# Stick-breaking attention: log(1+e^z) taken from e^z directly, with a cap, and the casts of two weight pieces moved from DVE to ACT

## The chip, the cores and the metric

The kernel runs on one core of a Trainium2 chip, in one launch. The metric is the device time of one execution in microseconds (us). Five engines matter: PE multiplies matrices and writes PSUM banks, ACT evaluates functions and copies, DVE and POOL do elementwise arithmetic (POOL on SBUF alone), and SP issues the DMA transfers. Each engine works through its own instructions in order.

## The reference, cut to what matters

One inference step of a two-layer trunk over 512 prompt frames and 64 sample frames, with a model width of 1024: first a convolution layer with its feed-forward part, then a layer of stick-breaking attention (16 query heads, 4 key/value heads) with its feed-forward part. The change lies in the attention:

```python
z = jnp.einsum('bgrqd,bgsd->bgrqs', q, k) * (HEAD_DIM ** -0.5)
mask = k_pos[None, :] < q_pos[:, None]
log_beta = jax.nn.log_sigmoid(z)
log_keep = jnp.where(mask, log_beta - z, 0.0)
after = lax.cumsum(log_keep, axis=4, reverse=True) - log_keep
att = jnp.where(mask, jnp.exp(log_beta + after), 0.0)
out = jnp.einsum('bgrqs,bgsd->bgrqd', att, v)
```

Here log_keep is -log(1+e^z), so every score needs s = log(1+e^z), then a sum of s over the later keys, then an exponential.

## The kernel before

Everything is float32. Matrices are multiplied as sums of two rounded parts: an operand x becomes hi (x rounded to the matrix engine's own 32-bit format, a copy or cast) and lo (x minus hi), and PE multiplies both. So each tensor that PE reads costs one cast and one subtraction.

The attention stage is cut into 10 pairs of heads (8 of prompt queries, 2 of sample queries), each pair into 2 units, each unit into 3 pieces of keys. That is 20 units and 60 pieces. In a prompt unit (16 of them) the pieces are 384 columns (in a 512-wide tile), 384 and 512 columns wide; in a sample unit (4 of them) they are 512, 512 and 256. A piece goes through these stages:

- `stage_z`: PE writes the scores z and the mask (-1e30) into one of five PSUM banks (L2105, L2110; tile `b`).
- `stage_s`: ACT and DVE make s in a buffer `t` (`zt` for the first prompt piece), L2130 to L2139; then `parts` makes hi and lo of it (tiles `s`, `zs`): the cast at L2070 on ACT, the subtraction at L2076 on DVE. For piece 0, POOL also adds two key blocks (`as`, L2154), which are split in turn (`a`).
- `stage_t`: PE adds the sums of s over later keys onto z in the same bank (L2177).
- `stage_e`: ACT takes the exponential (L2190) and the bank is free; then hi by a cast on DVE (L2072; tiles `e`, `ze`) and lo (L2076) on DVE for pieces 0 and 1 and on POOL for piece 2.
- `stage_v`: PE multiplies with the values (L2205); ACT and DVE collect the output `oc` (L2218, L2221).

Between these, PE has projections to do (L587): queries for later pairs (`pq`) and, late in the stage, the first half of the output projection (`pw`). Their weights arrive by SP (L309, buffers `wr`), and are split by ACT (L505) and DVE (L515). The split queries of a pair (`qd`, L1988 on ACT, L1992 on POOL) are spread over the partitions by SP: two transfers for the second unit (L2005) into a buffer whose last reader on PE has to be done, then one for the first unit (L2009).

The order on every engine is set by a planner (`Plan`). Each operation is entered with an engine, a cost and the keys that it reads and writes; a list scheduler places all of the section's operations and writes the instructions out in that order. So an operation that changes engine or goes away moves others on all engines of the section.

Of the kernel before, what the change touches and what calls it, by code (L numbers as in the profile page):

```python
# [6 lines left out]
AF = mybir.ActivationFunctionType  # L7
ALU = mybir.AluOpType
E = mybir.EngineType

P = 128
D = 1024
NC = D // P
SEQ = 512
# [59 lines left out]
LT, LV = 1, 2  # L74
W_LO = "DVE"
Q_LO = "Pool"
S_HI, E_HI = "ACT", "DVE"
E_LO = ("DVE", "DVE", "Pool")
A_LO = "Pool"

# [25 lines left out]
class Plan:  # L106
# [19 lines left out]
    def op(self, eng, cost, fn, reads=(), writes=(), lat=0.0, group=None, bias=0.0, urgent=False, port=False):  # L126
        i, deps = len(self.ops), set()
        for k in reads:
            if k in self.w:
                deps.add(self.w[k])  # L130
            self.r.setdefault(k, []).append(i)
        for k in writes:
            deps.update(self.r.pop(k, ()))
            if k in self.w:
                deps.add(self.w[k])
            self.w[k] = i
        deps.discard(i)
        self.ops.append((eng, cost, fn, deps, lat, group, bias, urgent, port or eng == "Pool"))
        self.end.append(0.0)
# [75 lines left out]
def build(tc, xT, vec, st, stp, bdp, wt, ck, cv, w_in, w_out, gu, down, wk, wv, wq, wo, yT, csp, css, kp, ks, vp, vs):  # L215
    nc = tc.nc
# [87 lines left out]
    X = {}  # L304
# [32 lines left out]
    op = plan.op  # L337
# [8 lines left out]
    def tile(key, tag, shape, dt=F32, pool=None):  # L346
        X[key] = (pool or cur[0]).tile(list(shape), dt, name="_".join(map(str, key)), tag=tag)
        return X[key]
# [4 lines left out]
    def act(n, scaled=True):  # L353
        return 0.186 + n * 0.000834 if scaled else 0.16 + n * 0.000715

    def dve(n, ptr=False):
        return n / 960 + (0.13 if ptr else 0.07)

    def pool(n):
        return 0.15 + n * 0.0021  # L360
# [4 lines left out]
    def both(k):  # L365
        return [k, (k, 0), (k, 1)]
# [187 lines left out]
    def eng(e):  # L554
        return nc.vector if e == "DVE" else nc.gpsimd

    def cst(e, n):
        return dve(n) if e == "DVE" else pool(n)
# [1287 lines left out]
    for t in range(2):  # L1846
        ft, ht, lt = (("ob0", "ob1", "ob2"), ("ob3", "ob0", "ob1"))[t]
        wi = take()
        tag = (("b0", "b1"), ("b2", "b3"))[t]
# [197 lines left out]
    def slot(q, first):  # L2047

        if first:

            i, j = turn["z" + q] % N_Z[q], turn["zt"] % N_Z["t"]
            turn["z" + q] += 1
            turn["zt"] += 1
            return ("z", q, i), f"z{q}{i}", ("z", "t", j), f"zt{j}"
        key, tag = (q, turn[q]), f"h{q}{turn[q] % N_HL[q]}"
        tk, tt = ("t", turn["t"]), (("sq1",) + tuple(f"t{i}" for i in range(N_T - 1)))[turn["t"] % N_T]
        turn[q] += 1
        turn["t"] += 1
        return key, tag, tk, tt

    def place(key, tag, shape, dt=F32):
        return X[key] if key[0] == "z" else tile(key, tag, (P, 5 * P) if tag == "sq1" else shape, dt, base if tag == "sq1" else None)

    def parts(key, tag, tk, tt, sl, le, he="DVE"):
        n = sl.stop - sl.start

        def hi():
            o = place(key, tag, (P, 2, 256 if key[0] == "a" else SEQ), F32R)[:, 0, sl]
            if he == "ACT":
                nc.scalar.activation(o, X[tk][:, sl], AF.Copy)  # L2070
            else:
                nc.vector.tensor_copy(o, X[tk][:, sl])  # L2072

        def lo():
            q = X[key]
            eng(le).tensor_tensor(q[:, 1, sl], X[tk][:, sl], q.bitcast(F32)[:, 0, sl], op=ALU.subtract)  # L2076

        if he == "ACT":
            op("ACT", act(n, False), hi, reads=[tt], writes=both(tag))
        else:  # L2080
            op("DVE", 0.08 + n / 1920, hi, reads=[tt], writes=both(tag), port=True)
        op(le, cst(le, n), lo, reads=[tt, (tag, 0)], writes=[(tag, 1)], port=True)
# [5 lines left out]
    def stages(un):  # L2088
# [30 lines left out]
        def cols(pi):  # L2119
            first = un.kind == "p" and pi == 0  # L2120
            sl = slice(P if first else 0, piece_cols(un.pieces[pi]))
            return first, sl, sl.stop - sl.start

        def stage_s(pi):
            first, sl, n = cols(pi)
            zz, zk = z[pi]
            key, tag, tk, tt = slot("s", first)

            def f():
                nc.scalar.activation(place(tk, tt, (P, SEQ))[:, sl], zz()[:, sl], AF.Abs)  # L2130

            def g():
                nc.scalar.activation(X[tk][:, sl], X[tk][:, sl], AF.Exp, scale=-1.0)

            def s():
                nc.scalar.activation(X[tk][:, sl], X[tk][:, sl], AF.Ln, bias=1.0)

            def v():
                nc.vector.scalar_tensor_tensor(X[tk][:, sl], zz()[:, sl], 0.0, X[tk][:, sl], op0=ALU.max, op1=ALU.add)  # L2139

            op("ACT", act(n, False), f, reads=[zk], writes=[tt])
            op("ACT", act(n, False), g, reads=["tbl"], writes=[tt])
            op("ACT", act(n, False), s, reads=["tbl"], writes=[tt])
            op("DVE", dve(n, True), v, reads=[zk], writes=[tt])
            parts(key, tag, tk, tt, sl, "DVE", S_HI)
            for (b, o, q0, q1) in un.pieces[pi]:
                sp.append((b, o, q0, q1, key, tag))
            if pi == 0:

                ak, atag, sk = ("a", turn["a"]), f"ha{turn['a'] % N_A}", ("as", turn["a"])  # L2150
                turn["a"] += 1

                def a():
                    nc.gpsimd.tensor_tensor(tile(sk, "as", (P, 256)), X[tk][:, 0:256], X[tk][:, 256:512], op=ALU.add)  # L2154

                op("Pool", pool(256), a, reads=[tt], writes=["as"])
                parts(ak, atag, sk, "as", slice(0, 256), A_LO)
                later.append((ak, atag))
# [25 lines left out]
        def stage_e(pi):  # L2184
            first, sl, n = cols(pi)
            zz, zk = z[pi]
            key, tag, tk, tt = slot("e", first)

            def f():
                nc.scalar.activation(place(tk, tt, (P, SEQ))[:, sl], zz()[:, sl], AF.Exp)  # L2190

            op("ACT", act(n, False), f, reads=[zk, "tbl"], writes=[tt])
            parts(key, tag, tk, tt, sl, E_LO[pi], E_HI)
            for (b, o, q0, q1) in un.pieces[pi]:
                at[pi].append((b, o, q0, q1, key, tag))

        def stage_v(pi):
# [30 lines left out]
            for (j, a, b, o) in jobs:  # L2228
# [24 lines left out]
                op("Pool", pool(b - a), lo, reads=[("oc", 0), ("oc", 1)], writes=[fk + (a,)])  # L2253

        return [stage_z, stage_s, stage_t, stage_e, stage_v]

    def prepare(i):
# [54 lines left out]
    n = len(todo)  # L2312
    fill = iter(range(NC))
    for s in range(n + LV):
        if 0 <= s - LT < n:
            st, pi, _, _ = todo[s - LT]
            st[2](pi)
            st[3](pi)
        if 0 <= s - LV < n:
            st, pi, _, _ = todo[s - LV]  # L2320
            st[4](pi)
        if s < n:
            st, pi, ahead, i = todo[s]
# [114 lines left out]
```

## Time and profile before

| what | value |
|---|---|
| time, median of 3 runs | 1265.24 us (1264.75 to 1266.52) |
| the profiled execution's own time | 1266.71 us |
| its span, first to last instruction | 1265.0 us |
| mean granted PE clock | 0.994 of full |
| busy over the span | PE 97%, DVE 79%, ACT 77%, POOL 60% |
| attention stage, first score matmul to the last values | 661.4 to 842.7 us |

The profile shows one execution. "Busy" counts time in which an engine has an instruction in work; matmuls overlap in PE's pipeline, so that a busy PE can still be short of instructions. A wait of an engine costs time only where that engine, or one behind it, sets the end.

### The profile page before, as it was taken

To read this page: it belongs to the slowest core of one execution; us is meant where nothing else is said; L and a number is where in the kernel's file an instruction comes from. 1 tells how busy PE (TensorE), PEld (TensorE's weight loads), DVE (VectorE), ACT (ScalarE), POOL (GpSimd) and SP (SyncE) were. 2 spreads that over 40 slices of the span, in tenths; PEclk is the share of its full clock that TensorE was granted. 3 is DMA by queue.
4 is the path that set the end of the run, shared out by engine and by line. 5 is a ranking of instruction groups with operands and counts; after the bars stand their busy time and mean duration, and the time that the engine had idled before them with its cause. 6 is when DMAs were issued, how large, how long until landed. Compare 5 with 4: busy or idle time off the path is not lost.

```text
span 1265.0 us, 24386 instructions
## 1 busy us (share of the span) xinstructions
PE 1229.3 (97%) x9018; PEld 1202.7 (95%) x9018; DVE 997.7 (79%) x1619; ACT 975.5 (77%) x1882; POOL 762.0 (60%) x638
## 2 busy tenths in 40 slices
PE   8999899999999999999999999999999999999996
PEld 7998889999999999999999989898999999999996
DVE  6997957977666659987789999999866666689976
ACT  6986236588878889687759999965988788896873
POOL 4988122459877777664304555555686777867633
PEclk9999999999999999999999999999999999999999
DMA  5333222132423323232363222231323233232322
GB/s 189 93 110 105 71 66 84 51 101 68 130 70 102 100 83 100 74 113 85 123 166 98 47 59 63 60 110 50 101 73 127 69 98 103 80 99 79 112 67 76
DMA packets 46455, 115.61 MB, mean 91 GB/s; under 512 B 8832, under 2 KB 18112, under 8 KB 46336
## 3 DMA queue, kind: packets, MB, share of 16 engines
q1 hardware_dynamic: 46336, 114.05, 29.6%
q8 instruction: 71, 1.16, 0.4%
q14 instruction: 48, 0.39, 0.1%
HBM read 99.04 MB, written 6.34 MB: 83 GB/s over the span
## 4 chain that ended last, share of the span: by engine, by line
PE 71%; DVE 8%; ACT 3%; issue 2%; POOL 2%; DMA 1%; DVEq 0%; SPq 0%; POOLq 0%; ACTq 0%
PE j_A L1396 26%; PE j_B L1396 13%; PE pd L587 7%; PE j_C L1396 6%; PE pq L587 4%; PE po L587 4%; PE b L2177 2%; PE pw L587 2%; PE b L2110 1%; PE b L2205 1%; PE pg L587 1%; PE pv L1925 1%; PE pk L587 1%; DVE wl L515 1%; DMA wr<-gu 1%
## 5 line engine op out<-in xcount | busy, mean ns | idle before, releaser
L505 ACT ACTIVATE wh<-wr 128x512 fp32r<-128x512 f32 (+1 forms) x303 | 183.2, 612 | 37.9 <-PE po L587 15.2
L515 DVE TENSOR_TENSOR wl<-wr,hp 128x512 fp32r<-128x512 f32 (+1 forms) x241 | 158.5, 662 | 53.1 <-ACT hp L510 52.5
L515 DVE TENSOR_TENSOR wl<-S,hp 128x512 fp32r<-128x512 f32 x226 | 152.4, 680 | 42.1 <-ACT hp L510 39.5
L505 ACT ACTIVATE wh<-S 128x512 fp32r<-128x512 f32 x228 | 140.8, 626 | 31.8 <-PE pd L587 10.4
L510 ACT ACTIVATE hp<-wr 128x512 fp32r<-128x512 f32 (+1 forms) x241 | 138.9, 578 | 30.6 <-DVE wl L515 30.1
L510 ACT ACTIVATE hp<-S 128x512 fp32r<-128x512 f32 x226 | 133.6, 594 | 13.9 <-POOL S L435 8.9
L435 POOL TENSOR_TENSOR S<-wr,wr 128x512 f32<-128x512 f32 x57 | 76.9, 1350 | 87.5 <-ACT wh L505 39.8
L471 POOL TENSOR_TENSOR S<-wr,S 128x512 f32<-128x512 f32 x57 | 78.4, 1377 | 32.4 <-DVE wl L515 18.0
L435 POOL TENSOR_TENSOR S<-wr 128x512 f32<-128x512 f32 x57 | 78.7, 1381 | 30.7 <-DVE wl L515 13.2
L1059 POOL TENSOR_TENSOR pacc<-pacc,pr 128x608 f32<-128x608 f32 x56 | 83.8, 1503 | 10.5 <-ACT pr L1056 3.9
L435 POOL TENSOR_TENSOR S<-S,wr 128x512 f32<-128x512 f32 x57 | 78.0, 1370 | 15.1 <-DVE wl L515 6.9
L1573 POOL TENSOR_TENSOR a<-a,r 128x576 f32<-128x576 f32 x44 | 66.9, 1522 | 15.6 <-DVE a L1550 15.6
L1573 POOL TENSOR_TENSOR t<-t,r 128x576 f32<-128x576 f32 x44 | 65.6, 1494 | 9.8 <-ACT t L1544 8.5
L587 PE MATMUL pd<-ap,wh 128*128 128x288 f32 x384 | 66.0, 294 | 0.0
L1579 DVE TENSOR_TENSOR a<-a,t 128x576 f32<-128x576 f32 x44 | 51.3, 1166 | 7.5 <-ACT t L1577 6.8
L587 PEld LDWEIGHTS pd<-ap,wh 128*128 128x128 f32 x384 | 56.0, 188 | 0.0
L515 DVE TENSOR_TENSOR wl<-wr,wh 128x512 fp32r<-128x512 f32 x62 | 48.5, 789 | 8.7 <-ACT wh L505 8.5
L1042 DVE SCALAR_TENSOR_TENSOR acc<-u,vecs,acc 128x608 f32<-128x608 f32 x60 | 51.1, 852 | 1.0
L1544 ACT ACTIVATE t<-j_A 128x288 f32<-128x288 f32 x84 | 34.0, 405 | 21.9 <-PE j_A L1396 21.5
L934 PE MATMUL py<-vt,wm 128*128 128x152 f32 x288 | 41.3, 307 | 5.2 <-DVE ye L944 5.2
L934 PEld LDWEIGHTS py<-vt,wm 128*128 128x128 f32 x288 | 40.4, 201 | 6.0 <-DVE ye L944 5.8
L1056 ACT ACTIVATE pr<-u,vecs 128x608 f32<-128x608 f32 x56 | 42.9, 793 | 3.9 <-POOL pacc L1059 3.8
(859 smaller groups left out, 4567.7 us busy)
## 6 DMA issues: line engine op xcount, KB each, us to landing
wr<-gu SPq DMA_DIRECT2D x88, 512.0 KB, 3.4
wr<-down SPq DMA_DIRECT2D x32, 512.0 KB, 3.7
wr<-w_in SPq DMA_DIRECT2D x15, 512.0 KB, 3.9
wr<-down SPq DMA_DIRECT2D x16, 384.0 KB, 3.1
qd<-qd SPq DMA_DIRECT2D x21, 256.0 KB, 3.5
wr<-w_out SPq DMA_DIRECT2D x8, 512.0 KB, 3.5
wr<-wq SPq DMA_DIRECT2D x8, 512.0 KB, 3.7
wr<-wo SPq DMA_DIRECT2D x16, 256.0 KB, 2.6
```

The source lines that it names most:

```text
L435: eng(e).tensor_tensor(t[:, :n], x[1](), y[1](), op=ALU.subtract if sub else ALU.add)
L471: eng(e).tensor_tensor(v[:, :n], X[("raw", i0)][:, n : 2 * n], v[:, :n], op=ALU.subtract)
L505: nc.scalar.activation(X[("w", u)][0][:, :n], get(), AF.Copy)
L510: nc.scalar.activation(t[:, :n], get(), AF.Copy)
L515: eng(le).tensor_tensor(b[:, :n], get(), a.bitcast(F32)[:, :n], op=ALU.subtract)
L587: nc.tensor.matmul(o[hf], (hi, hi, lo)[j][:, s], (xh, xl, xh)[j], start=(start and q == 0 and j == 0), stop=(stop and q == n - 1 and j == 2),)
L934: nc.tensor.matmul(X[("py", c)][:, YO + q * QW : YO + q * QW + QW], X[("wm", c, q)][:, Q * j : Q * j + Q, :].rearrange("p j d -> p (j d)") ...
L1042: nc.vector.scalar_tensor_tensor(dst, src, wt_, dst, op0=ALU.mult, op1=ALU.add)
L1059: nc.gpsimd.tensor_tensor(X[("pacc", c)], X[("pacc", c)], X[("pr", c, i)], op=ALU.add)
L1396: nc.tensor.matmul(out, a[:, s], b, start=(start and q == 0 and i == 0), stop=(q == len(ops_) - 1 and i == 2), skip_group_check=True,)
L1573: nc.gpsimd.tensor_tensor(X[k], X[k], r, op=ALU.mult)
L1579: op("DVE", dve(T), lambda: nc.vector.tensor_tensor(X[ku], X[ku], X[kg], op=ALU.mult), reads=by_part(tg), writes=by_part(tu), port=True)
```

## The change

Before, s was formed as max(z, 0) + log(1 + e^-|z|), with ACT passes for the absolute value, for the exponential and for the logarithm. Now ACT takes e^z straight from the bank, then log(1 + e^z), and DVE forms max(min(that, 15), z). The DVE instruction stays one instruction of the same kind with its inputs exchanged. Second, the casts of the attention weights (hi of `e`) go to ACT for pieces 0 and 1 and stay on DVE for piece 2. The casts of s stay on ACT.

```diff
--- before.py
+++ after.py
@@ -74,7 +74,9 @@
 LT, LV = 1, 2
 W_LO = "DVE"
 Q_LO = "Pool"
-S_HI, E_HI = "ACT", "DVE"
+S_HI = ("ACT", "ACT", "ACT")
+E_HI = ("ACT", "ACT", "DVE")
+SOFT = 15.0
 E_LO = ("DVE", "DVE", "Pool")
 A_LO = "Pool"
 
@@ -2126,23 +2128,20 @@
             zz, zk = z[pi]
             key, tag, tk, tt = slot("s", first)
 
+
             def f():
-                nc.scalar.activation(place(tk, tt, (P, SEQ))[:, sl], zz()[:, sl], AF.Abs)
-
-            def g():
-                nc.scalar.activation(X[tk][:, sl], X[tk][:, sl], AF.Exp, scale=-1.0)
+                nc.scalar.activation(place(tk, tt, (P, SEQ))[:, sl], zz()[:, sl], AF.Exp)
 
             def s():
                 nc.scalar.activation(X[tk][:, sl], X[tk][:, sl], AF.Ln, bias=1.0)
 
             def v():
-                nc.vector.scalar_tensor_tensor(X[tk][:, sl], zz()[:, sl], 0.0, X[tk][:, sl], op0=ALU.max, op1=ALU.add)
-
-            op("ACT", act(n, False), f, reads=[zk], writes=[tt])
-            op("ACT", act(n, False), g, reads=["tbl"], writes=[tt])
+                nc.vector.scalar_tensor_tensor(X[tk][:, sl], X[tk][:, sl], SOFT, zz()[:, sl], op0=ALU.min, op1=ALU.max)
+
+            op("ACT", act(n, False), f, reads=[zk, "tbl"], writes=[tt])
             op("ACT", act(n, False), s, reads=["tbl"], writes=[tt])
             op("DVE", dve(n, True), v, reads=[zk], writes=[tt])
-            parts(key, tag, tk, tt, sl, "DVE", S_HI)
+            parts(key, tag, tk, tt, sl, "DVE", S_HI[pi])
             for (b, o, q0, q1) in un.pieces[pi]:
                 sp.append((b, o, q0, q1, key, tag))
             if pi == 0:
@@ -2190,7 +2189,7 @@
                 nc.scalar.activation(place(tk, tt, (P, SEQ))[:, sl], zz()[:, sl], AF.Exp)
 
             op("ACT", act(n, False), f, reads=[zk, "tbl"], writes=[tt])
-            parts(key, tag, tk, tt, sl, E_LO[pi], E_HI)
+            parts(key, tag, tk, tt, sl, E_LO[pi], E_HI[pi])
             for (b, o, q0, q1) in un.pieces[pi]:
                 at[pi].append((b, o, q0, q1, key, tag))
 
```

The planner then orders the attention stage anew. Ahead of the stage and behind it the instructions stand as before, but for a few casts and projection blocks at its edges (line numbers shift by 2).

On DVE, early in the stage, around the first casts of the weights, before (`zt`, `t` are work buffers, `q` the queries):

```order
L2139 SCALAR_TENSOR_TENSOR zt_7935<-b_8486,zt_7935 128x384
L2072 CAST ze_7934<-zt_7936 128x384
L2076 TENSOR_TENSOR ze_7934<-zt_7936,ze_7934 128x384
L1974 SCALAR_TENSOR_TENSOR q_8625<-pq_0_8510,r 128x288
L1974 SCALAR_TENSOR_TENSOR q_8625<-pq_1_8511,r 128x288
L2076 TENSOR_TENSOR zs_7933<-zt_7935,zs_7933 128x384
L2072 CAST e_8645<-t_8634 128x384
L2072 CAST a_8648<-as_8610 128x256
L2076 TENSOR_TENSOR e_8645<-t_8634,e_8645 128x384
L2139 SCALAR_TENSOR_TENSOR t_8607<-b_8353,t_8607 128x384
```

The same place on DVE after the change:

```order
L517 TENSOR_TENSOR wl_8599<-wr_8397,wh_8598 128x512
L2078 TENSOR_TENSOR zs_7933<-zt_7935,zs_7933 128x384
L2078 TENSOR_TENSOR ze_7934<-zt_7936,ze_7934 128x384
L2139 SCALAR_TENSOR_TENSOR t_8623<-t_8623,b_8567 128x384
L2074 CAST a_8647<-as_8604 128x256
L2078 TENSOR_TENSOR s_8649<-t_8623,s_8649 128x384
L2139 SCALAR_TENSOR_TENSOR t_8645<-t_8645,b_8473 128x512
L2074 CAST e_8676<-t_8666 128x512
L2078 TENSOR_TENSOR e_8669<-t_8634,e_8669 128x384
```

The casts of `ze` and of the 384-column `e` are gone from DVE; the subtraction behind each stays, and now reads what ACT has cast. The cast of the 512-column `e` (piece 2) is still there.

On PE, before the scores of the first prompt pair behind the first sample pair (`qd_9363` are its queries, `kst` the keys, `sums` the triangular matrices), before:

```order
L587 MATMUL pq_0_9451<-xh_80_8214,wh_8948 128x288
L587 MATMUL pq_1_9452<-xh_80_8214,wh_8948 128x288
L587 MATMUL pq_0_9451<-xl_80_8215,wh_8948 128x288
L587 MATMUL pq_1_9452<-xl_80_8215,wh_8948 128x288
L587 MATMUL pq_0_9451<-xh_80_8214,wl_8949 128x288
L587 MATMUL pq_1_9452<-xh_80_8214,wl_8949 128x288
L2177 MATMUL b_8478<-a_9416,sums 128x256 x2
L2177 MATMUL b_8478<-s_9418,sums 128x256 x4
L2177 MATMUL b_8478<-s_9445,sums 128x256 x2
L2105 LDWEIGHTS identb
L2105 MATMUL b_8451<-mask,identb 128x256
L2110 MATMUL b_8451<-qd_9363,kst_7919 128x256 x4
```

The same place on PE after the change (its queries are `qd_9339`):

```order
L589 MATMUL pq_0_9388<-xh_80_8324,wl_9147 128x288
L589 MATMUL pq_1_9389<-xh_80_8324,wl_9147 128x288
L2112 MATMUL b_8567<-qd_9163,kst_7918 128x256 x2
L589 MATMUL pq_0_9388<-xh_80_8334,wh_9146 128x288
L589 MATMUL pq_1_9389<-xh_80_8334,wh_9146 128x288
L589 MATMUL pq_0_9388<-xl_80_8335,wh_9146 128x288
L589 MATMUL pq_1_9389<-xl_80_8335,wh_9146 128x288
L589 MATMUL pq_0_9388<-xh_80_8334,wl_9147 128x288
L589 MATMUL pq_1_9389<-xh_80_8334,wl_9147 128x288
L2107 LDWEIGHTS identb
L2107 MATMUL b_8473<-mask,identb 128x256
L2112 MATMUL b_8473<-qd_9339,kst_7919 128x256 x4
```

Before, one query projection block (6 matmuls `pq`) stands between the last score matmuls of the sample pair's first unit, after which a buffer is refilled for this pair, and these scores; now seven blocks (42) do, of which the rows show the end.

On SP, in the second half of the stage, before (L2005 and L2009 spread queries, L309 loads weights):

```order
L2005 DMA qd_9397<-qd_9363 64x1024 x2
L2009 DMA qd_9363<-qd_9363 64x1024
L309 DMA wr_9510<-wo 128x512
L2005 DMA qd_9606<-qd_9570 64x1024 x2
L2009 DMA qd_9570<-qd_9570 64x1024
L309 DMA wr_9734<-wo 128x512
L2005 DMA qd_9846<-qd_9819 64x1024 x2
L2009 DMA qd_9819<-qd_9819 64x1024
```

The same stretch on SP after the change (L2007 and L2011 spread queries, L311 loads weights):

```order
L311 DMA wr_9494<-wo 128x512
L311 DMA wr_9519<-wo 128x512
L2007 DMA qd_9577<-qd_9531 64x1024 x2
L2011 DMA qd_9531<-qd_9531 64x1024
L311 DMA wr_9633<-wo 128x512
L311 DMA wr_9773<-wo 128x512
L2007 DMA qd_9843<-qd_9733 64x1024 x2
L311 DMA wr_9859<-wo 128x512
L2011 DMA qd_9733<-qd_9733 64x1024
```

Two weight loads now stand ahead of each of these two spreads, and one stands between the two parts of the second (L2007 and L2011). A load between the two parts happens at two spreads of the stage; before, it happened at none.

## Rows read from the trace of the kernel before

**Rows 1.** Busy us of each engine (instructions) before, in and behind the attention stage.

```profile
0.00:661.40 661.40, 646.35 (x4742) 635.96 (x4742) 505.57 (x782) 481.59 (x885) 390.23 (x337) 0.99 0.32 99
661.40:845.00 183.60, 178.07 (x1253) 165.17 (x1252) 176.62 (x333) 166.88 (x354) 99.84 (x94) 1.00 0.26 66
845.00:1265.00 420.00, 404.89 (x3027) 401.53 (x3025) 315.48 (x506) 327.07 (x643) 271.93 (x208) 0.99 0.28 90
```

**Rows 2.** The same by stretches: length, PE, PEld, DVE, ACT, POOL, PE clock, DMA.

```profile
680.00:700.00 20.00, 20.00 (x140) 18.32 (x140) 19.04 (x33) 19.14 (x41) 11.72 (x12) 1.00 0.19 41
700.00:720.00 20.00, 19.97 (x137) 18.44 (x136) 19.10 (x37) 19.26 (x44) 12.02 (x12) 1.00 0.27 61
720.00:740.00 20.00, 17.60 (x119) 15.75 (x118) 19.94 (x37) 19.50 (x43) 10.69 (x11) 1.00 0.23 53
740.00:760.00 20.00, 19.75 (x145) 18.48 (x146) 19.22 (x37) 18.35 (x42) 9.88 (x10) 1.00 0.28 66
800.00:820.00 20.00, 18.28 (x137) 17.18 (x136) 19.80 (x38) 17.84 (x39) 8.70 (x8) 1.00 0.30 71
820.00:845.00 25.00, 24.18 (x174) 23.02 (x173) 24.81 (x52) 17.57 (x35) 15.98 (x15) 1.00 0.23 70
```

**Rows 3.** PE's groups by form, 661 to 845 us: first and last of 19.

```profile
L587 PE MATMUL pw<-ob,wh 128*128 128x288 f32 x141 | 24.6, 296 | 0.0
...
L2105 PE MATMUL b<-mask,identb 128*128 128x256 bf16 x20 | 5.6, 279 | 2.8 <-ACT t L2190 2.7
```

**Rows 4.** The chain that ended last: start us, us, what.

```profile
650.37 11.20 PE pq L587 x84
...
731.16 1.46 POOL qd L1992
732.64 0.48 SPq L2005
733.16 3.67 DMA qd<-qd
736.90 2.88 DMA qd<-qd
739.83 0.73 PE b L2110 x4
```

**Rows 5.** DVE's casts of the weights in the stage: busy us, mean ns.

```profile
L2072 DVE CAST e<-t 128x512 fp32r<-128x512 f32 x24 | 12.6, 533 | 0.2 <-ACT t L2190 0.2
...
L2072 DVE CAST ze<-zt 128x384 fp32r<-128x384 f32 x16 | 8.5, 532 | 1.2 <-ACT zt L2190 0.6 <-PE b L2205 0.6
...
L2072 DVE CAST e<-t 128x384 fp32r<-128x384 f32 x16 | 7.3, 458 | 0.0
```

**Rows 6.** The casts of L2072 on DVE: min/median/max ns.

```profile
L2072 DVE CAST e<-t x44: 286/414/1653, 674.5 to 838.0; 128x512 fp32r<-128x512 f32 x24, 128x384 fp32r<-128x384 f32 x16, 128x256 fp32r<-128x256 f32 x4
```

**Rows 7.** ACT's groups in the stage: busy us, mean ns of one, idle before.

```profile
L2133 ACT ACTIVATE t<-t 128x512 f32<-128x512 f32 (+2 forms) x44 | 24.6, 570 | 0.2
L2130 ACT ACTIVATE t<-b 128x512 f32<-128x512 f32 (+2 forms) x44 | 23.3, 537 | 3.2 <-PE b L2110 2.0 <-DVE s L2076 0.9
L2190 ACT ACTIVATE t<-b 128x512 f32<-128x512 f32 (+2 forms) x44 | 23.0, 535 | 3.0 <-PE b L2177 2.3 <-POOL e L2076 0.6 <-DVE e L2076 0.2
L505 ACT ACTIVATE wh<-wr 128x512 fp32r<-128x512 f32 x23 | 14.2, 628 | 1.3 <-PE pw L587 1.2
...
L2133 ACT ACTIVATE zt<-zt 128x384 f32<-128x384 f32 x16 | 8.4, 524 | 0.1
...
L2070 ACT ACTIVATE zs<-zt 128x384 fp32r<-128x384 f32 x16 | 8.3, 521 | 0.0
```

**Rows 8.** Who waited for whom, 655 to 850 us: total us, times, longest us.

```profile
PE b L2105 <- ACT t L2190: 2.7, 4, 1.7
...
DVE s L2076 <- ACT s L2070: 1.7, 4, 0.5
```

**Rows 9.** What SP's queue waited for, 640 to 850 us: total, times, longest.

```profile
SPq L309 <- DVE wl L515: 73.9, 18, 8.9
```

## The prediction

> **What bounds the kernel now.** I first read the busy time by stage. PE is busy for 178.07 of the 183.60 us of the attention stage, DVE for 176.62 and ACT for 166.88 [rows 1]. So all three are nearly full there, and PE's own work is the least that the stage can take. The change touches no other stage, so the question is how much of the stage PE spends waiting, and for whom.
>
> Two readings bound that. By the busy time PE is idle for 183.60 - 178.07 = 5.5 us. That is too little, since matmuls overlap in the pipeline and a late one hides. The other reading counts the work. The 19 groups of matmuls in the stage, of which the first and the last are shown [rows 3], hold 1256 matmuls with 374,912 columns in all (count times width, added up). Undisturbed, 84 matmuls of 288 columns took 11.20 us [rows 4], that is 133 ns each or 0.463 ns a column. 374,912 x 0.463 = 173.6 us of work, in 184 us: 10.4 us without work. So between 5.5 and 10.4 us can be had here, and no more, as long as PE does the same matmuls.
>
> Then I looked for the place of the waits, by stretches of the stage [rows 2]. Three stretches lose PE time: 720 to 740 us (2.40 of 20), 800 to 820 (1.72 of 20) and 820 to 845 (0.82 of 25). In the same three DVE is full: 19.94, 19.80 and 24.81 us. In the three others shown DVE is at 19.04 to 19.22 of 20, and PE loses 0.00, 0.03 and 0.25 us. The clock is granted in full in all of them. So PE runs dry where DVE has no slack left. The reader should see that 96% of DVE is harmless and 99% is not: pieces pile up in front of it until PE has used up its projections.
>
> **What the change takes away and adds.** There are 60 pieces, 20 each of numbers 0, 1 and 2.
>
> On ACT one pass per piece goes. The remaining exponential reads the PSUM bank, as the absolute value did. From a bank, the absolute value takes 537 ns and the exponential 535 ns in the same mix of sizes [rows 7], so this exchange costs nothing. What goes is the exponential within SBUF, L2133: 24.6 + 8.4 = 33.0 us [rows 7]. What comes is 40 casts: 32 of 384 columns at 521 ns, which is the price of the like cast of s, and 8 of 512 columns at 628 ns, the price of the like cast of weights [rows 7]. That is 16.7 + 5.0 = 21.7 us. ACT falls by 11.3 us, from 166.9 to 155.6.
>
> On DVE 40 casts go: the 16 of `ze` (8.5 us), the 16 of `e` with 384 columns (7.3 us), and 8 of the 24 with 512 columns at 533 ns (4.3 us) [rows 5]. That makes 20.1 us. It is the upper bound, because these durations hold delays: the casts of `e` have a median of 414 ns and a longest of 1653 ns [rows 6]. If the delays only move to other instructions, 40 x 0.414 = 16.6 us go. DVE comes to 156.5 to 160.0 of 183.6 us. I take the first, since a delay goes with the instruction that has it. The instruction that joins s with z stays one pass with its inputs exchanged. No row shows it in this form. The least is no change; as the most I take the excess of mean over median of the cast, 533 - 414 = 119 ns, on all 60: 7.1 us. Even then DVE does 13.0 us less than now. I take nothing for it, since the sizes and the number of inputs are the same.
>
> The subtraction behind each moved cast must now wait for another engine. The nearest row is the same hand-over for s: over 60 of them DVE waited 1.7 us in all, at most 0.5 at once [rows 8]. 40 more give 1.1 us. They cost nothing while DVE has other work in hand; with 20 us less to do it has idle time for them. Queued behind such a subtraction are the joins and subtractions of the next pieces, for which PE's sums wait.
>
> A piece's way through its bank gets shorter by one pass of 570 ns [rows 7], so the bank comes free earlier. PE waited 2.7 us for banks that the second exponential had not freed, in 4 waits [rows 8].
>
> The planner also moves PE's fillers. The loss at 720 to 740 us ends with a chain that no lighter DVE shortens: POOL's part of the queries 1.46 us, SP 0.48, two transfers of 3.67 and 2.88 us in a row, then the scores at 739.83 [rows 4]. Between the release of that buffer and these scores PE had 6 projection matmuls and now has 42. The 36 more are 36 x 133 ns = 4.8 us of cover, against 2.40 us lost. No matmul is added, so this only takes cover from places that did not need it.
>
> The Trainium skill, in its page "ScalarE: Activation LUTs", section "Rules for kernel authors", sends simple elementwise work to VectorE instead of ScalarE. That speaks against moving casts. By that rule alone the casts are dearer than before; this trace agrees on the price of one (521 against 414 ns), and the second rival below says what would come of it.
>
> **The sum.** With DVE at 156.5 of 183.6 us (85%), the stage should look like the three stretches where DVE has slack: 0.28 us of PE lost in 60 us, so 0.9 us in the stage. Of the 5.5 us of visible idle time, 4.6 come back. Of the hidden 10.4 - 5.5 = 4.9 us, I cannot say from a row how much is waiting and how much is the pace of mixed matmuls, so none and all are the bounds, and I take half, 2.4 us. Together 7.0 us. The profiled execution took 1266.71 us, of which 1265.0 are its span and 1.7 lie around it; it would take 1259.7. The median of the runs is 1.5 us lower, and gives 1265.24 - 7.0 = **1258.2 us**. With all the hidden time it is 1254.8, with none 1260.6: this case's own range.
>
> **The rivals.**
>
> PE's waits are not DVE's making. The three losing stretches could lose to the spread of queries and to hand-overs, with DVE full by coincidence. For it speaks the chain at 731 to 740 us, which is POOL, SP and transfers [rows 4]. Against it speaks that the two other losing stretches have DVE at 99% too, and that the spread now has more cover. Then only the loss at the end of the stage, 0.8 us, comes back: 1264.4 us.
>
> ACT's dearer casts land on the way. Each moved cast takes 521 instead of 414 ns and stands in ACT's queue ahead of exponentials that free banks. If all 40 delay PE by the difference, and the hand-overs too, 40 x 0.107 + 1.1 = 5.4 of the 7.0 us are lost: 1263.6 us. Against it: ACT as a whole falls from 91% to 85% of the stage.
>
> SP gets in the way, and the kernel gets slower. At two spreads a weight load now stands between the transfers for the second unit and the one for the first, in the order shown for SP. A load waits until DVE has split the buffer's last content; the longest such wait was 8.9 us [rows 9]. The last transfer would wait for the earlier ones anyway, 3.67 us [rows 4]. That leaves 5.2 us at each place, 10.5 at both: 1258.2 + 10.5 = 1268.7 us. It decides from 3.5 us a place on, that is when the split ends 7.2 us or more after the first transfers start. Against it: most of the 73.9 us in these waits are a queue that is early, not DVE that is late [rows 9], and DVE gets lighter.
>
> **Chances and range.** The forecast 0.72; waits not of DVE's making 0.14; ACT's casts 0.05; SP 0.09. The first holds because three stretches agree on one sign. About 0.2%, or 2.5 us, is what a measurement of this kernel can tell from no change: below 1262.7 is faster, above 1267.8 slower. Faster is the forecast and 0.04 of the second case, where a part of the idle time comes back: 0.76. Same is the rest of it, ACT's case, and 0.01 of SP's where one place is covered: 0.16. Slower 0.08. The range goes from the lower bound of the forecast, 1254.5 with a little for rounding, up past ACT's case to 1264.0; it leaves out SP's case and 0.1 of the second.
>
> **What the profile after would show.** Right: DVE busy in the stage at 156 to 164 us and ACT at about 156; no stretch with DVE at 99%; PE's idle time in the stage near 1 us; the last matmul with the values some 7 us earlier; the stages before and behind as long as now. The step on ACT is wrong if an exponential from a bank is not near 535 ns; the step on DVE if the joining instruction has grown, or the subtractions take up what the casts leave. The prediction fails as a whole if DVE gets its slack and PE still waits, which would show in the same places as waits for transfers or for ACT.

## The result, and the profile after

The changed kernel takes 1257.03 us (median of 5 runs, 1254.52 to 1257.78) against 1265.24 us. The ratio is 0.9924, with a 95% interval of 0.9913 to 0.9936: 8.2 us faster in the medians, 9.6 us (8.1 to 11.0) by the ratio. The profiled execution took 1257.46 us with a span of 1255.7 us, 9.3 us under the span before.

The stages of the profile after, with the columns of [rows 1]; the last matmul with the values now ends at 833.3 instead of 842.7 us, so the stage is cut at 836:

```profile
0.00:661.40 661.40, 648.37 (x4754) 638.75 (x4754) 506.81 (x785) 482.12 (x885) 388.95 (x337) 0.99 0.33 100
661.40:836.00 174.60, 173.15 (x1244) 163.28 (x1243) 161.21 (x290) 157.65 (x335) 94.58 (x94) 1.00 0.27 65
836.00:1255.70 419.70, 404.77 (x3024) 401.23 (x3023) 316.97 (x506) 326.04 (x642) 271.46 (x208) 0.99 0.29 91
```

The gain lies in the attention stage: what stands behind it takes as long as before. PE's idle time in the stage went from 5.5 to 174.60 - 173.15 = 1.45 us. Counted as in the prediction, its 22 groups of matmuls hold 372,320 columns, at 0.463 ns each 172.4 us of work in 175 us: 2.6 us without work, against 10.4.

The stretches of the stage after, with the columns of [rows 2]:

```profile
700.00:720.00 20.00, 18.83 (x131) 17.40 (x130) 17.71 (x31) 17.73 (x40) 10.37 (x10) 1.00 0.29 64
720.00:740.00 20.00, 20.00 (x151) 19.28 (x150) 18.96 (x34) 18.64 (x40) 11.64 (x11) 1.00 0.22 52
740.00:760.00 20.00, 20.00 (x152) 18.88 (x152) 19.94 (x35) 18.84 (x42) 11.46 (x11) 1.00 0.36 92
...
800.00:820.00 20.00, 20.00 (x153) 19.18 (x152) 19.72 (x36) 18.90 (x40) 8.51 (x10) 1.00 0.20 48
```

PE no longer loses anything at 720 to 740 or at 800 to 820 us. But the reader should see the row of 740 to 760 us: DVE is full again, 19.94 of 20 us, and PE loses nothing. A full DVE alone does not make PE wait. The one loss left inside, at 700 to 720 us, is a spread of queries, as the chain of that stretch shows (start us, us, what):

```profile
699.83 5.31 DMA qd<-qd
...
705.20 2.84 DMA qd<-qd
...
708.09 0.74 PE b L2112 x4
```

The groups of the stage after that answer to [rows 5, 7]: of DVE, then of ACT (two fences, since they are two views).

```profile
L2139 DVE SCALAR_TENSOR_TENSOR t<-t,b 128x512 f32<-128x512 f32 x24 | 16.3, 680 | 0.7 <-ACT t L2136 0.6
...
L2078 DVE TENSOR_TENSOR e<-t,e 128x384 fp32r<-128x384 f32 x16 | 12.6, 787 | 0.1
...
L2078 DVE TENSOR_TENSOR ze<-zt,ze 128x384 fp32r<-128x384 f32 x16 | 10.6, 662 | 0.9 <-ACT ze L2072 0.7 <-PE b L2176 0.2
```

```profile
L2133 ACT ACTIVATE t<-b 128x512 f32<-128x512 f32 x24 | 14.3, 594 | 2.9 <-PE b L2112 2.6
...
L2072 ACT ACTIVATE ze<-zt 128x384 fp32r<-128x384 f32 x16 | 8.4, 526 | 0.4 <-PE b L2204 0.3
L2072 ACT ACTIVATE e<-t 128x384 fp32r<-128x384 f32 x16 | 8.4, 522 | 0.1
...
L2072 ACT ACTIVATE e<-t 128x512 fp32r<-128x512 f32 x8 | 4.8, 632 | 0.5 <-PE b L2204 0.5
```

The casts on ACT cost 21.6 us, the joining instruction on DVE is as long as it was (680 ns for 512 columns, before and after), and the subtractions behind the moved casts have grown. So has one that is behind none of them: that of `s` with 384 columns went from 573 to 758 ns in the mean.

### The profile page after: what moved, and what is told of

Its sections match the earlier page's. It is cut to its first block, busy times and chain, and to the rows that moved or that the text cites. A ratio compares the mean times of both kernels' runs of the same rounds, so it can differ in the third digit from the quotient of the medians.

```text
span 1255.7 us, 24378 instructions
## 1 busy us (share of the span) xinstructions
PE 1226.3 (98%) x9018; PEld 1203.3 (96%) x9018; DVE 985.0 (78%) x1579; ACT 965.8 (77%) x1862; POOL 755.0 (60%) x638
## 4 chain that ended last, share of the span: by engine, by line
PE 78%; DVE 6%; issue 1%; ACT 1%; POOL 1%; DMA 1%; DVEq 0%; SPq 0%; POOLq 0%; ACTq 0%
PE j_A L1398 28%; PE j_B L1398 14%; PE j_C L1398 7%; PE pd L589 7%; PE pq L589 4%; PE po L589 4%; PE b L2176 4%; PE pw L589 2%; PE b L2112 2%; PE b L2204 2%; PE pg L589 1%; PE pv L1927 1%; PE pk L589 1%; DVE wl L517 1%; DVE xs L1498 1%
## 5 line engine op out<-in xcount | busy, mean ns | idle before, releaser
L517 DVE TENSOR_TENSOR wl<-wr,wh 128x512 fp32r<-128x512 f32 x62 | 51.3, 836 | 9.1 <-ACT wh L507 8.9
```

What stands on the lines that cost most here:

```text
L517: eng(le).tensor_tensor(b[:, :n], get(), a.bitcast(F32)[:, :n], op=ALU.subtract)
```

## The experiments

The theory of the prediction was that lighter engines, DVE above all, take PE's waits away. The rival that the result left standing was that the planner's new order does it, with its cover for the spread of queries: the two came together in one change. A second question was which of the two edits counts. All kernels were timed in 5 rounds; the kernel before took 1265.7 to 1265.9 us beside them. The table has for each the attention stage from the first mask matmul to the last with the values, in its profile: length, PE's idle time in it, and the busy shares of DVE and ACT (the row of the changed kernel is that of the result).

| kernel | us | ratio to before (95%) | stage us | PE idle us | DVE | ACT |
|---|---|---|---|---|---|---|
| before | 1265.24 | 1 | 181.3 | 5.5 | 96% | 91% |
| changed | 1257.03 | 0.9924 (0.9913 to 0.9936) | 171.9 | 1.5 | 92% | 91% |
| e1 new log alone | 1264.06 | 0.9988 (0.998 to 0.9997) | 174.8 | 2.4 | 96% | 82% |
| e2 casts alone | 1273.13 | 1.0064 (1.005 to 1.0078) | 188.8 | 9.3 | 88% | 96% |
| e3 new work, old order | 1265.74 | 1.0007 (0.9999 to 1.0016) | 180.3 | 5.0 | 89% | 87% |
| e4 old work, new order | 1277.62 | 1.0099 (1.0085 to 1.0113) | 191.0 | 14.1 | 91% | 89% |
| e5 all casts on ACT | 1257.76 | 0.9936 (0.9922 to 0.995) | 174.2 | 1.6 | 90% | 95% |
| e6 new order, casts on DVE | 1269.45 | 1.0032 (1.0019 to 1.0045) | 182.3 | 6.9 | 96% | 78% |
| e7 new order, third pass | 1280.02 | 1.0115 (1.0101 to 1.0129) | 193.4 | 17.4 | 81% | 96% |
| e8 changed, other plan | 1259.26 | 0.9952 (0.9939 to 0.9965) | 173.1 | 1.8 | 95% | 90% |
| e8 before, other plan | 1267.43 | 1.0012 (1.0003 to 1.0021) | 182.3 | 6.6 | 97% | 91% |
| e9 changed, one round | 1262.47 | 0.9967 (0.9955 to 0.998) | 175.7 | 3.0 | 94% | 89% |
| e9 before, one round | 1269.55 | 1.0028 (1.0018 to 1.0038) | 184.1 | 9.5 | 95% | 90% |

The stage lengths are not of quite the same work, since a plan can move query projections over the stage's edge: it holds 1236 matmuls in the kernel before, in e3, in e5 and in e8 before, 1242 in e2, and 1223 or 1224, some 1.6 us less than 1236, in the others.

### e1 and e2: one edit alone, planned anew

e1 is the changed kernel with

```diff
-E_HI = ("ACT", "ACT", "DVE")
+E_HI = ("DVE", "DVE", "DVE")
```

> Only the log(1+e^z) part; all casts of the weights stay on DVE, and the planner orders the stage for that. ACT loses 60 passes (33 us of the stage), DVE keeps its 177 us. If DVE's load made PE wait, this gives little: 1262 to 1265 us, with DVE still at 99% in stretches where PE loses time. If ACT's passes, or the length of a piece's way through its bank, made PE wait, it gives most of the gain: 1257 to 1259 us.

Measured: 1264.06 us, 1.6 us under the 1265.66 of the kernel before beside it. DVE kept its 96% of the stage. So the new logarithm alone is worth little, as the theory of DVE's load said. The sign that went with it did not come: where PE loses time, 1.10 us at 720 to 740 and 0.81 at 780 to 800, DVE is at 98% and 95%, not at 99%. And the stage is shorter than the time tells. The profiled execution, the longest of the eleven, has a span 7.4 us over that of the changed kernel. Of these, 1.9 us lie ahead of the stage, where PE has the same matmuls in both, 2.9 in the stage and 2.6 behind it. Behind it PE still waited for DVE: 2.7 us in four waits between 838 and 877 us, against 1.2 us in two waits of the changed kernel in a like stretch.

e2 is the kernel before with

```diff
-S_HI, E_HI = "ACT", "DVE"
+S_HI, E_HI = "ACT", ("ACT", "ACT", "DVE")
```

and the choice by piece at the call of `parts`.

> Only the casts of pieces 0 and 1 moved to ACT; the absolute value and the two further passes stay. DVE loses about 16 us, ACT gains 21.7 us, to about 188 us of work in a stage of 184 us. If DVE's load was the cause alone: 1258 to 1261 us. If ACT counts as well: ACT becomes the bound and the stage gets longer by its excess over PE's work, 188 against 174: 1270 to 1280 us.

Measured: 1273.13 us, 7.5 us slower, in the range expected if ACT counts as well. ACT has 180.4 us of work in this stage (some 188 expected), more than PE's 173. That this sets the stage's length is argued: PE's named waits for its scores, sums and values end on DVE for 3.7 us and on ACT for 2.3, and the granted clock fell to 0.91 at 740 to 760 us in this execution. So the casts alone cost, and the new logarithm is what makes room for them.

### e3 and e4: the work and the order apart

In e3 the planner is given the operations and costs of the kernel before, and only what they issue is changed (rows cut from the diff; DVE's joining instruction is exchanged as in the change):

```diff
-AF.Abs)                    # the pass that reads the bank
+AF.Exp)
-nc.scalar.activation(X[tk][:, sl], X[tk][:, sl], AF.Exp, scale=-1.0)
+pass
-            if he == "ACT":
+            if (do or he) == "ACT":    # do: ACT, ACT, DVE by piece
```

PE, POOL and SP have the rows of the kernel before, one by one. e4 is the opposite: planned as the changed kernel, with the old passes and all weight casts issued on DVE.

> The changed work in the order of the kernel before: the planner is given the old operations and costs, so PE, POOL and SP have the very order of before, and the casts and the exponential are issued where the old operations stood. If the lighter engines are the cause: within 2 us of the changed kernel, 1256 to 1259 us. If the new order (more projections as cover at the spread of queries) is the cause: near the kernel before, 1263 to 1265 us, with the loss at 720 to 740 us still there.

> The old work (absolute value, three ACT passes, weight casts on DVE) in the order that the planner makes for the changed work: PE, POOL and SP have the very order of the changed kernel. If the order is the cause: 1257 to 1259 us. If the lighter engines are: near the kernel before, 1264 to 1267 us, or over it, since the order was made for lighter engines.

Measured: 1265.74 and 1277.62 us. This is where the theory of load fell, at least as it stood. With the lighter work in the old order nothing is gained, though DVE has fallen to 89% and ACT to 87% of the stage. The loss at 720 to 740 us is still there, as was expected for the order as the cause. Here are the stretches of e3:

```profile
720.00:740.00 20.00, 17.86 (x120) 15.68 (x119) 19.63 (x32) 18.59 (x39) 11.26 (x11) 1.00 0.24 53
740.00:760.00 20.00, 19.00 (x140) 17.74 (x140) 16.91 (x31) 16.90 (x39) 8.48 (x9) 1.00 0.25 64
...
800.00:820.00 20.00, 18.83 (x145) 18.07 (x145) 18.20 (x36) 15.66 (x34) 9.34 (x9) 1.00 0.32 81
```

PE loses 2.14 us at 720 to 740 (before 2.40), where DVE is still at 98%, and 1.17 at 800 to 820 (before 1.72), with DVE at 91%; and 1.00 at 740 to 760 with DVE at 85%. The chain of e3 at the first place is that of [rows 4], within half a microsecond:

```profile
730.73 1.47 POOL qd L1994
732.22 0.48 SPq L2007
...
732.74 3.65 DMA qd<-qd
736.45 2.87 DMA qd<-qd
...
739.37 0.73 PE b L2112 x4
```

Removing 5 of 37 DVE instructions there did not make the queries ready earlier (the scores start at 739.37 us against 739.83, in a stage that began 1.1 us earlier), and the old order has one block of projections to cover them. Further back the chain does hang on DVE, and there on ACT. POOL came to its part only after a wait for DVE's cast of `e`, as long as before (2.78 us), and DVE had itself stood idle for ACT's cast of `zs` (timelines of POOL and of DVE in e3: start, us, what, and in brackets the idle time before it and who ended it):

```profile
728.26 1.30 POOL L2078 TENSOR_TENSOR e<-t,e 128x512 fp32r<-128x512 f32 x1 [2.80 <-DVE e L2074]
```

```profile
715.22 0.56 DVE L2078 TENSOR_TENSOR zs<-zt,zs 128x384 fp32r<-128x384 f32 x1 [1.01 <-ACT zs L2072]
```

ACT's cast of `zs`, at 714.67 us, stands directly behind a moved cast, that of `ze` at 714.25. So at this place what DVE gained went into a wait for ACT, which had been given that cast.

But the order is not the cause by itself either: under the old work the new order is 12 us worse than the old one, which fits the "or over it" of the expectation. PE then waits for banks, 7.2 us in 11 waits for the second exponential (PE's waits in e4: total, times, longest):

```profile
PE b L2108 <- ACT t L2191: 7.2, 11, 1.3
```

So the gain is neither of the two alone. The lighter work allows an order that the old work cannot keep up with.

### e6 and e7: which load the new order needs light

Both have the rows of the changed kernel on PE, POOL and SP. e6 issues the weight casts on DVE; e7 issues the absolute value and the third pass, with the old joining instruction (rows cut from the diffs):

```diff
 # e6
-            if he == "ACT":
+            if (do or he) == "ACT":    # do = "DVE" for the weights
 # e7
-AF.Exp)                    # one pass that reads the bank
+AF.Abs)
+nc.scalar.activation(X[tk][:, sl], X[tk][:, sl], AF.Exp, scale=-1.0)
```

> The order of the changed kernel (PE, POOL and SP row by row), its short way to log(1+e^z), but all weight casts executed by DVE where the order has them on ACT. DVE has the load of before, ACT is some 33 us lighter than before. If DVE's load is what the new order needs light: well over the changed kernel, 1263 to 1270 us. If ACT's load or the shorter way through the bank is what it needs: 1256 to 1260 us.

> The order of the changed kernel, the casts on ACT as there, but the absolute value and the third ACT pass of before are executed, so that ACT has about 188 us of work in the stage and every piece stays some 0.6 us longer on its way to the sums. If ACT's load or the way's length is what the new order needs: 1272 to 1285 us. If DVE's load alone is: 1257 to 1262 us.

Measured: 1269.45 and 1280.02 us, 12.4 and 23.0 us over the changed kernel. Both loads count. In e7 PE waits for banks again, and longer:

```profile
PE b L2107 <- ACT t L2190: 12.0, 13, 2.5
```

Here ACT has 185.9 us of work in a stage of 193.4. e7 both loads ACT and lengthens a piece's way; these two were not told apart. Nor was a third thing in e3, e4 and e6: a cast that is issued on another engine than the plan's stands in that engine's queue at the place planned for the first, and what the place costs beside the load is not known.

### e8 and e9: other orders for the same work

To see how much of a time is the luck of one order, both kernels were planned twice more. In e8 each hand-over between engines is taken as 0.1 us longer in the attention stage, in e9 the planner makes one pass instead of eight:

```diff
 # e8, in both kernels
+    plan.TO = {e: v + 0.1 for e, v in Plan.TO.items()}
     flush()
+    plan.TO = Plan.TO
 # e9, in both kernels
+    plan.ROUNDS = 1
     flush()
+    plan.ROUNDS = Plan.ROUNDS
```

> The changed work, in another order: for the attention stage the planner takes every hand-over between engines as 0.1 us longer. If the lighter work lets any plan of this planner do well, this is near the changed kernel: 1255 to 1260 us. If the changed kernel's order is a lucky one, it falls anywhere between 1257 and 1268 us.

> The work of the kernel before, planned with the same longer hand-overs. If the old work sets the time and the plan little: 1263 to 1268 us. If the kernel before lost its 9 us of waits to an unlucky order: below 1261 us.

> The changed work in a third order: for the attention stage the planner makes a single pass in place of eight and takes what it finds first. If the lighter work does well under any plan: 1255 to 1261 us; if the plan decides: 1262 to 1270 us.

> The work of the kernel before in a third order, from a single pass of the planner. If the old work sets the time: 1264 to 1270 us. Whatever the plan, at least 3 us over the changed work under the same planner setting, if the work is the cause; within 2 us of it, if the order is.

Measured: 1259.26 against 1267.43, and 1262.47 against 1269.55 us. The order moves the time by up to 5.4 us for the changed work and up to 4.3 us for the old, but the difference at the same planner setting is 8.2, 8.2 and 7.1 us. So the gain is that of the work, provided the stage is planned for it, at each of three settings of the planner. The plan counts as well: 1262.47 us lies in the range that stood for "the plan decides", and the changed kernel's own order is the best of its three, as is that of the kernel before. No order tried brings the old work under 1265 us.

### e5: the casts of the last piece on ACT as well

```diff
-E_HI = ("ACT", "ACT", "DVE")
+E_HI = ("ACT", "ACT", "ACT")
```

> The changed kernel with the casts of piece 2 moved to ACT as well, planned anew. ACT gains 16 casts of 512 columns and 4 of 256, some 11.7 us, and comes to about 169 us in the stage, against PE's 173. If ACT near PE's own work is harmless: 1255 to 1258 us. If ACT needs slack as the earlier runs on ACT's load suggest: 1260 to 1266 us.

Measured: 1257.76 us, no different from the changed kernel by the intervals. ACT is at 164.9 us in a stage of 174.2, 95%, and PE idles 1.6 us. So ACT's casts are harmless at this level, and there is nothing more to have from this side: PE's work fills the stage.

## Why the prediction was right, and where it was not

**The forecast** of 1258.2 us was 1.2 us high, the gain 7.0 instead of 8.2 us (9.6 by the ratio). That PE's waits in the attention stage were the whole of it, and 10.4 us the most to be had, held. Of the signs that were to show it, DVE's 156 to 164 us, PE's idle time near 1 us and the unchanged stage behind came true; "no stretch with DVE at 99%" did not. One end of the forecast's own range was added up wrongly: with 4.6 us of visible and all of the hidden time it is 1255.7, not 1254.8.

**The visible part** of the sum: 4.6 of 5.5 us were to come back, 4.1 did. The size was right, but the rule that gave it, that DVE at 85% would leave PE hardly a wait, was not: DVE is at 92% of the stage. That much is luck. **The hidden part** is the term that was mis-sized: half of 4.9 us was assumed, and 2.6 - 1.45 = 1.15 us are left, so 3.75 came back. Most of what the busy time hid was waiting and not the pace of mixed matmuls. Together 7.8 us in the stage; the profile's 9.3 has 12 matmuls more done ahead of the stage (4754 against 4742 up to 661.4 us), 1.6 us. That they took no longer there belongs to this execution: the eight profiles with these matmuls ahead come to the stage at 660.0 to 664.0 us.

**ACT.** The casts came to 21.6 us (21.7 forecast), and the exponential from a bank to the price of the absolute value (594 against 594 ns for 512 columns). ACT's busy time over the whole span fell by 9.7 us, from 975.53 to 965.81, not by 11.3, for a reason given under DVE. ACT's casts on the way, the second rival, did not show in an order made for them: e5 puts still more there at no cost. In the old order it shows, at 714 us of e3.

**DVE.** From 176.62 to 161.21 us are 15.4 us, not 20.1, and the window has 43 instructions fewer, not 40. Over the whole span, 1619 against 1579 instructions, it is 997.66 against 985.00: 12.7 us. (In the other runs with these 40 casts on ACT it is 979 to 992 us, in those with them on DVE 995 to 1001.) So even the lower bound, 16.6, was too high.

Two steps failed here. One is that durations were added up as if they stood end to end. In the stage before, DVE starts an instruction 77 ns before the one ahead of it ends (median of 286 overlaps; 105 ns on ACT, of 268), so that 40 casts free 40 x 0.077 = 3.1 us less than their rows say. Added up as durations, DVE's work fell by 15.7 us over the span, and ACT's by 11.2. The other step is "a delay goes with the instruction that has it", which is the rest, some 4 us. The subtraction of `ze` took 546 ns in the mean before and 662 after; its longest was 559 ns and is 1660 now, while the cast ahead of it, which is gone, had been up to 1450 ns. The joining instruction with its inputs exchanged costs nothing, as taken.

**The mechanism.** "PE runs dry where DVE has no slack left" failed as a statement about places. A stretch of the kernel before that the prediction did not show, 780 to 800 us, lost 0.30 us with DVE at 94%. After the change DVE is at 99.7% in one stretch and PE loses nothing there; in e3 PE loses at 800 to 820 us with DVE at 91%, and at 740 to 760 with DVE at 85%. What the runs put in its place: each order of the stage needs DVE and ACT to be light enough to keep up, and the waits sit where the order leaves no cover. With ACT at 96% (e2) the planner's order leaves PE idle for 9.3 us of the stage, and under the old work for 5.5 to 9.5; with both engines at 95% or less it finds one that loses 1.5 to 3.0. With DVE at 96% and ACT at 82% (e1) it is 2.4, within that range; e1 loses in part behind the stage, where DVE is late. Why lighter engines do not help within the old order was seen at one place only, the spread of queries at 731 us, where the chain runs over POOL, SP and transfers, and before those over DVE and ACT with a moved cast on the way. The prediction had taken that chain for one that a lighter DVE does not shorten; its start on POOL did wait for DVE, but DVE then waited for ACT. That it is the same at the other places was not tried.

**The rivals.** The first, that the waits are not DVE's making, had more in it than its 0.14: for a fixed order it is what e3 shows (1265.74 us, 1264.4 forecast for that case), but the change comes with a new order. The cover of 42 projections held: the stretch at 720 to 740 us loses nothing. SP's weight loads between the transfers cost nothing. At the two spreads that have one, at 682.53 and 763.94 us, the last transfer is issued 4.25 and 4.28 us after the first; at the other prompt spreads it is 4.19 to 5.88. SP's queue after the change waited for DVE's splits no longer than before (total, times, longest),

```profile
SPq L311 <- DVE wl L517: 64.9, 18, 8.4
```

against 73.9 and 8.9 us [rows 9], and PE's only wait for queries, at 708 us, is at a spread without such a load.

## What to carry to other kernels

Where a planner writes the order, an edit's gain cannot be read off the old order's waits: try the new work in the old order and the old work in the new one, and replan both kernels under a changed setting, before giving the gain to either. In a stage where three engines are nearly full, take the pass away that makes room first and move work into that room after: either step alone gave 1.6 us or cost 7.5, both together gave 8.2. Look for idle time of a pipelined engine by counting its work as well as by its busy time, which here hid almost half of it. And take an engine's rows as more than the time that removing them frees: its instructions overlap, and a delay need not go with them.

## What the runs showed of the hardware that was not expected

Delays on DVE stayed when the delayed instructions went. In the stage before (661 to 845 us), 37 of the 224 DVE instructions whose tensor inputs all lie in SBUF took over 250 ns longer than the median of their operation and size, 25.4 us in all. After the change (661 to 836 us) it is 35 of 181, and 22.4 us. `ze` is an example: its cast had taken 428 ns in the median and up to 1450; the subtraction behind it, which had never taken more than 559 ns, now takes up to 1660 at a median of 552. But a delay does not simply pass to the next instruction: in e3, where that cast is gone too, the subtraction stayed within 559 ns.

Each of the delayed instructions in the two traces ran beside a POOL instruction, for at least 0.39 us; of the others 88 of 187 before, and 74 of 146 after, ran beside one at all. The instructions with an input in a PSUM bank, 110 in each trace, never took more than 16 ns over their median, though 77 and 75 of them ran beside POOL as well; the joining instruction took at most 693 ns before and 691 after. That POOL is the cause was not tested, since no run changes POOL's work.
